# SwiGLU's upward products of two blocks in seven half-depth products instead of eight

## The chip, the cores and the metric

One Trainium2 chip, one core. The time is device microseconds of one launch; the median of three runs of the kernel before is 3152.8 us (3152.46 to 3155.65). Names as in the profile: PE is TensorE, DVE VectorE, ACT ScalarE, POOL GpSimd, SP the engine that issues most transfers.

## The reference, cut to what matters

A trunk of two layers; each layer has a SwiGLU, a mixer, and a second SwiGLU, so four SwiGLUs in all. 576 time steps (512 of the prompt and 8 x 8 samples), width 1024, inner width 2816 = 22 blocks of 128.

```
def swiglu(h, w1, w3, w2):
    return (jax.nn.silu(h @ w1) * (h @ w3)) @ w2
...
h = modulate(rms_norm(x, w['g_ffn1']), sh1, sc1)
x = x + 0.5 * gt1 * swiglu(h, w['w1_a'], w['w3_a'], w['w2_a'])
```

All is float32. The change is in h @ w1 and h @ w3, the upward products.

## The kernel before, in words

A float32 product is made of three matmuls on values split in two: hi (rounded to the engine's short form) and lo (the rest); hi x hi, hi x lo, lo x hi (`three`, lines 203 to 212). The time axis lies in two halves of 288 columns (HB), so one matmul is 128 x 128 weights by 128 x 288 of h, and `run` (line 214) adds the 8 depth tiles of one half in one bank.

Weights come block by block: `pump` (line 123) issues the transfer of a raw tile (128 x 1024, three in flight, line 142), casts it to hi on ScalarE (line 161), and puts off the subtraction that gives lo to VectorE (line 121, `rest`). WB = 5 split tiles may live at a time, AHEAD = 4 sets how early a tile is split. The order of use is a list of steps with their keys, filled by `ffn`; transfers are issued in the order of the keys.

`pair_step` takes one block: for each time half, w1's product, w3's product, then `post`: silu on ScalarE (line 611), the multiply on VectorE (line 612), and the split of the result g into hi and lo (lines 225 and 226). The blocks go in three groups (GROUPS: 6, 8 and 8); behind each group, `down` multiplies its g with the rows of w2 that belong to it, eight tiles of output, and adds to x (lines 581, 584, 587, 590). Between the steps of the first two SwiGLUs stand the units that make the conditioning values (`ada_unit`, line 277), two behind each block until they are used up. `end` takes the last four downward tiles, with the next normalization's statistics between them, and `begin` the first two blocks of a SwiGLU. Each engine works through its own queue in the order in which the program was written down.

Of the kernel before, what the change touches and what calls it, by code (L numbers as in the profile page):

```python
# [21 lines left out]
FT = 22  # L23
GROUPS = ((0, 6), (6, 8), (14, 8))
# [5 lines left out]
RAW, WB, AHEAD, ADA = 3, 5, 4, 12  # L30
# [5 lines left out]
SLOTS, TEMPS = 38, 12  # L36
# [26 lines left out]
class Trunk:  # L63
    def __init__(self, nc, tc, d, o, ctx):
        self.nc, self.tc, self.d, self.o = nc, tc, d, o
        pool = lambda name, **k: ctx.enter_context(tc.tile_pool(name=name, **k))
        self.cp = pool("const", bufs=1)
        self.wp = pool("weights", bufs=1)
        self.sp = pool("slots", bufs=SLOTS)
        self.tp = pool("temps", bufs=TEMPS)  # L70
        self.pp = pool("psum", bufs=1, space=PSUM)
        self.dp = pool("dram", bufs=1, space=bass.MemoryType.DRAM)
        self.n = 0
        self.steps = []
        self.spare = set()
        self.bg = deque()
        self.taps = 3
        self.later = []
        self.quota = 0
        self.ada_sb = None  # L80
# [29 lines left out]
    def start(self):  # L110
        self.keys = [k for ks, _ in self.steps for k in ks]
        self.at = {k: i for i, k in enumerate(self.keys)}
        assert len(self.at) == len(self.keys)
        self.order = np.cumsum([k[0] not in ("ada", "do") for k in self.keys]).tolist()
        self.raw, self.late, self.split = deque(), deque(), {}
        self.n_dma = self.held = self.whole = self.live = self.cur = 0
# [6 lines left out]
    def pump(self, later=False):  # L123
        nc = self.nc
        while True:
# [5 lines left out]
            elif self.n_dma < len(self.keys) and self.keys[self.n_dma][0] == "ada":  # L131
                if self.whole < ADA and self.n_dma <= self.cur + 2 * ADA:
# [14 lines left out]
            if self.raw and self.quota and self.order[self.raw[0][0]] <= self.order[self.cur] + AHEAD:  # L147
                key = self.keys[self.raw[0][0]]
                spare = key in self.spare
                if spare or self.live < WB:  # L150
# [17 lines left out]
            if not went:  # L168
                return

# [58 lines left out]
    def setup(self):  # L229
# [4 lines left out]
        self.one512 = cp.tile([128, 128], F32, name="one512")  # L234
# [10 lines left out]
        nc.gpsimd.memset(self.one512, 1.0 / 512)  # L245
# [181 lines left out]

    def end(self, keys, xs, post, last):
# [13 lines left out]
        for i, (k, w) in enumerate(zip(keys, ws)):  # L442
            ps = self.run(w, xs, 1, 0, {0: 4, 1: 6}.get(i), {0: stats, 1: spread}.get(i))
# [25 lines left out]
    def begin(self, l, sh, pairs, post):  # L469
# [24 lines left out]
        for pair in pairs:  # L494
            ps = self.outer([self.use(k) for k in pair], 1)
            for k in pair:
                self.free(k)
            self.pump()
            post(pair, 1, ps)
# [98 lines left out]
    def ffn(self, l, ab, sh, fill, first, last):  # L598
# [23 lines left out]
        if not first:  # L622
            self.spare |= {pairs[0][1], pairs[1][0]}

        def opening():
            if first:
                self.begin_first(l, sh, pairs[0], post)
            else:
                self.begin(l, sh, pairs[:2], post)
# [11 lines left out]

        def down(keys, final):
            f0, n = GROUPS[keys[0][3]]
# [14 lines left out]
        for gi, (f0, n) in enumerate(GROUPS):  # L658
            for f in range(f0, f0 + n):
# [4 lines left out]
                elif f > 1 or first:  # L664
                    self.steps.append((pairs[f], lambda f=f: pair_step(pairs[f])))
                    add_fill(0 if first and f == 5 else 2)
            final = gi == 2
# [12 lines left out]
    def mixer(self, l, last):  # L680
# [290 lines left out]
        def norm():  # L971
# [7 lines left out]
            for half in range(2):  # L979
                c = slice(half * HB, (half + 1) * HB)  # L980
                ps = self.mis(HB)
                nc.tensor.matmul(ps, self.one512, a[:, c], start=True, stop=True)
                for i in range(4):
                    nc.vector.tensor_sub(cvs[i][:, c], cvs[i][:, c], ps)
# [436 lines left out]
```

## Time and profile before

| | |
|---|---|
| median of three runs | 3152.8 us |
| profiled execution | 3153.93 us |
| its span | 3152.2 us |
| granted TensorE clock, mean | 0.993 |
| TensorE matmuls | 23412, busy 98% |
| VectorE, ScalarE, GpSimd busy | 49%, 28%, 13% |
| read from HBM | 328.9 MB, 108 GB/s over the span |

The busy share of TensorE is made of overlapping matmuls: one is listed at 0.29 us, and they follow each other every 0.13 us. What a matmul costs is therefore read from how many are issued in a stretch without waits, not from its duration.

### The profile page before, as it was taken

The page shows a single profiled execution, that of the slowest core. Times are in us where ns is not written, and L with a number is a line of the kernel's source. Part 1 is how long each engine was busy: PE and PEld are TensorE (multiplying, and loading weights), DVE is VectorE, ACT ScalarE, POOL GpSimd, SP SyncE. Part 2 cuts the span into 40 slices and gives each one's busy share as a digit, 9 for nine tenths or more (in the row PEclk, how much of TensorE's full clock was granted, in tenths as well). Part 3 has the DMA queues.
Part 4 walks back from the last instruction along what each step waited for, and adds up shares of the span by engine and source line. Part 5 has one row for each costly group of instructions (what it writes and reads, how often), then busy time and mean ns, then how long its engine had stood idle before and what let it go on. Part 6 is the DMA issues. An engine that isn't in the chain of part 4 may idle for free.

```text
span 3152.2 us, 55303 instructions
## 1 busy us (share of the span) xinstructions
PE 3096.1 (98%) x23412; PEld 2972.5 (94%) x23412; DVE 1533.6 (49%) x2840; ACT 874.4 (28%) x1468; POOL 407.0 (13%) x526
## 2 busy tenths in 40 slices
PE   7999999999999999999999999999999999999998
PEld 5999999899998999999999999988999899999998
DVE  5333335355995463323363333454679854533334
ACT  4222223222232342222232222332223333422221
POOL 1000004223212020000020000042221220200000
PEclk9999999999999999999999999999999999999999
DMA  7544424325322334636322222233352233222221
GB/s 275 166 154 151 151 88 129 111 68 124 86 75 69 119 121 146 207 126 218 109 79 79 84 87 85 84 123 111 83 113 86 70 101 92 75 89 81 81 82 57
DMA packets 142680, 349.67 MB, mean 111 GB/s; under 512 B 32400, under 2 KB 36752, under 8 KB 142432
## 3 DMA queue, kind: packets, MB, share of 16 engines
q1 hardware_dynamic: 135776, 329.35, 33.2%
q0 software_dynamic: 5504, 15.61, 1.8%
q8 instruction: 183, 3.00, 0.4%
q10 hardware_dynamic: 1152, 1.18, 0.1%
q14 instruction: 65, 0.53, 0.1%
HBM read 328.90 MB, written 12.45 MB: 108 GB/s over the span
## 4 chain that ended last, share of the span: by engine, by line
PE 95%; POOL 2%; DVE 1%; DMA 1%; ACT 0%; issue 0%; ACTq 0%; SPq 0%; POOLq 0%; DVEq 0%
PE pl L210 29%; PE pl L211 28%; PE pl L212 28%; PE pm L277 2%; PE pl L765 1%; PE pl L767 1%; PE pl L766 1%; PE pm L1164 1%; PE pm L1166 1%; DMA ada<-in_ada 1%; DVE hl L383 0%; DVE t L393 0%; PE pm L350 0%; DMA x<-in_x 0%; PE pm L1145 0%
## 5 line engine op out<-in xcount | busy, mean ns | idle before, releaser
L211 PE MATMUL pl<-hl,hi 128*128 128x288 f32 x4576 | 1348.9, 295 | 11.0 <-POOL hl L421 9.6
L210 PE MATMUL pl<-hh,hi 128*128 128x288 f32 x4576 | 1358.7, 297 | 0.3 <-ACT hh L419 0.2
L212 PE MATMUL pl<-hh,lo 128*128 128x288 f32 x4576 | 1348.1, 295 | 0.0
L210 PEld LDWEIGHTS pl<-hh,hi 128*128 128x128 f32 x4576 | 858.9, 188 | 21.5 <-DVE t L612 10.7
L211 PEld LDWEIGHTS pl<-hl,hi 128*128 128x128 f32 x4576 | 859.0, 188 | 13.8 <-POOL hl L421 10.9
L212 PEld LDWEIGHTS pl<-hh,lo 128*128 128x128 f32 x4576 | 858.8, 188 | 0.0
L121 DVE TENSOR_TENSOR lo<-raw,hi 128x1024 fp32r<-128x1024 f32 (+1 forms) x446 | 551.5, 1238 | 517.5 <-ACT hi L161 517.3
L161 ACT CAST hi<-raw 128x1024 fp32r<-128x1024 f32 (+1 forms) x446 | 459.1, 1032 | 849.9 <-PE pl L211 639.4
L210 PE MATMUL pl<-ghi,hi 128*128 128x288 f32 x1408 | 419.5, 298 | 0.0
L212 PE MATMUL pl<-ghi,lo 128*128 128x288 f32 x1408 | 414.7, 295 | 0.0
L211 PE MATMUL pl<-glo,hi 128*128 128x288 f32 x1408 | 414.6, 294 | 0.0
L590 POOL TENSOR_TENSOR xs<-xs,t 128x64 f32<-128x64 f32 x112 | 42.2, 377 | 1831.8 <-DVE t L587 1831.6
L210 PEld LDWEIGHTS pl<-ghi,hi 128*128 128x128 f32 x1408 | 264.1, 188 | 13.6 <-issue 11.5
L612 DVE TENSOR_TENSOR t<-t,pl 128x288 f32<-128x288 f32 x176 | 79.9, 454 | 404.8 <-PE pl L212 390.2
L211 PEld LDWEIGHTS pl<-glo,hi 128*128 128x128 f32 x1408 | 264.2, 188 | 0.0
L212 PEld LDWEIGHTS pl<-ghi,lo 128*128 128x128 f32 x1408 | 264.1, 188 | 0.0
L210 PE MATMUL pl<-s,hi 128*128 128x288 f32 x768 | 229.3, 299 | 0.0
L211 PE MATMUL pl<-s,hi 128*128 128x288 f32 x768 | 227.9, 297 | 1.1 <-DVE s L226 1.1
L212 PE MATMUL pl<-s,lo 128*128 128x288 f32 x768 | 227.8, 297 | 0.0
L957 DVE SCALAR_TENSOR_TENSOR cv<-up,vec,cv 128x512 f32<-128x512 f32 x240 | 209.2, 872 | 5.4
L225 ACT CAST ghi<-t 128x288 fp32r<-128x288 f32 x176 | 76.1, 432 | 481.0 <-DVE t L612 481.0
L210 PEld LDWEIGHTS pl<-s,hi 128*128 128x128 f32 x768 | 145.8, 190 | 3.3 <-issue 1.5
(197 smaller groups left out, 2689.2 us busy)
## 6 DMA issues: line engine op xcount, KB each, us to landing
ada<-in_ada SPq DMA_DIRECT2D x288, 256.0 KB, 4.5
raw<-in_win SPq DMA_DIRECT2D x120, 512.0 KB, 3.6
raw<-in_w1a SPq DMA_DIRECT2D x44, 512.0 KB, 3.6
raw<-in_w3a SPq DMA_DIRECT2D x44, 512.0 KB, 3.7
raw<-in_w1b SPq DMA_DIRECT2D x44, 512.0 KB, 3.6
raw<-in_w3b SPq DMA_DIRECT2D x44, 512.0 KB, 3.6
raw<-in_w2a SPq DMA_DIRECT2D x32, 512.0 KB, 3.5
raw<-in_w2b SPq DMA_DIRECT2D x32, 512.0 KB, 3.5
```

The lines of the kernel that those rows point to most:

```text
L121: self.nc.vector.tensor_sub(lo, t, hi.bitcast(F32))
L161: nc.scalar.copy(hi[:, :m], t[:, c])
L210: mm(ps[:, :HB], hi[:, c], x[0][:, t], start=first, stop=False)
L211: mm(ps[:, :HB], hi[:, c], x[1][:, t], start=False, stop=False)
L212: mm(ps[:, :HB], lo[:, c], x[0][:, t], start=False, stop=last)
L225: nc.scalar.copy(hi, src)
L277: nc.tensor.matmul(self.ps_ada[32 * j:32 * j + 32, :], self.cs[:, k], w, start=(k == 0), stop=(k == 7))
L590: nc.gpsimd.tensor_add(xs, xs, t[:].rearrange("p b t -> p (b t)"))
L612: nc.vector.tensor_mul(s, s, ps[1][:, :HB])
L765: mm(ps, xh, wh, start=(k == 0), stop=False)
L766: mm(ps, xh, wl, start=False, stop=False)
L957: nc.vector.scalar_tensor_tensor(cv[:, :S], up[:, k:k + S], w[:, k:k + 1], cv[:, :S], ALU.mult, ALU.add)
```

## The change

From the fifth block on, two blocks f and f + 1 are taken together, first for w1 and then for w3. Of the 2 x 2 scheme (two blocks by two halves of the depth, two halves of the depth by two halves of time) seven products of half the depth are made instead of eight (`seven`). For that the weights' quarters are summed on GpSimd (`sums`): from the raw tiles a and b come X (a itself), S (half as wide), Y and Z, and each is split into hi and lo like a weight tile before. The sums and differences of h are made once in each SwiGLU (`forms`, and `last_forms` just before the first pair of blocks, which writes over h's second time half of the first four depth tiles). The seven results are joined by VectorE on the way out. w1's four results stay in four temporaries until the w3 step. The silu's multiply is on VectorE for one of the four results and on GpSimd for three.

The groups are now four (6, 6, 4, 6 blocks), raw tiles four instead of three, temporaries 10 instead of 12, slots 37 instead of 38, and conditioning tiles in flight 4 instead of 12 once the start is over. A block of ones that held 1/512 is gone; its factor is applied on VectorE.

```
-GROUPS = ((0, 6), (6, 8), (14, 8))
+GROUPS = ((0, 6), (6, 6), (12, 4), (16, 6))
-RAW, WB, AHEAD, ADA = 3, 5, 4, 12
+RAW, WB, AHEAD, ADA, ADA_LATER = 4, 5, 4, 12, 4
-SLOTS, TEMPS = 38, 12
+SLOTS, TEMPS = 37, 10
...
+            if self.jobs:
+                if not (later and once) and self.live + self.jobs[0][0] <= WB:
+                    self.jobs.popleft()[1]()
+                    if not later:
+                        self.rest()
+                    went = once = True
...
+    def halves(self, key, t, n=1024):
+        w = [self.wp.tile([128, 1024], F32R, tag=x, bufs=WB, name=self.name(x)) for x in ("hi", "lo")]
+        self.live += 1
+        self.nc.scalar.copy(w[0][:, :n], t[:, :n])
+        self.late.append((w[1][:, :n], t[:, :n], w[0][:, :n]))
+        self.split[key] = w
+    def sums(self, key, a, b):
+        add = self.nc.gpsimd.tensor_add
+        s = self.wp.tile([128, 512], F32, tag="s1", bufs=1, name=self.name("s1"))
+        add(s, b[:, :512], b[:, 512:])
+        add(b[:, :512], b[:, :512], a[:, :512])
+        def z():
+            self.rest()
+            add(a[:, :512], a[:, :512], s)
+            add(a[:, 512:], a[:, 512:], a[:, :512])
...
+        self.jobs.extend(((1, lambda: self.halves((*key, "X"), a)), (0, z),
+                          (1, lambda: self.halves((*key, "S"), s, 512)), (1, yh), (1, zh)))
...
+    def last_forms(self):
+        for i, z in enumerate(self.zs):
+            hi, lo = self.T[7][i]
+            self.nc.scalar.copy(hi, z[:, HB:])
+            self.nc.vector.tensor_sub(lo, z[:, HB:], hi.bitcast(F32))
...
+    def seven(self, key, post):
...
+        p, q = bank(), bank()
+        product(p, "X", 0, quarter(0, 0), True, True)
+        s1 = self.temp([128, HB])
+        nc.scalar.copy(s1, p)
+        self.rest()
+        product(q, "Y", 0, self.T[7], True, True)
+        u, v = self.temp([128, HB]), s1
+        nc.vector.tensor_add(u, s1, q)
+        self.rest()
+        product(p, "X", 1, quarter(1, 0), False, True)
+        free("X")
+        post(0, 0, p)
+        self.rest()
+        product(q, "Z", 0, self.T[2], False, True)
+        nc.vector.tensor_sub(v, s1, q)
+        nc.vector.tensor_sub(u, u, q)
+        self.rest()
+        r = bank()
+        product(r, "S", 0, self.T[5], True, True)
+        free("S")
+        post(1, 1, v, r)
+        self.rest()
+        t = bank()
+        product(t, "Y", 1, self.T[4], True, True)
+        free("Y")
+        post(1, 0, v, t)
+        self.rest()
+        product(r, "Z", 1, quarter(1, 1), False, True)
+        free("Z")
+        post(0, 1, u, r)
+        self.rest()
...
+            def up3(i, j, a, b=None):
+                s = acts.pop((i, j))
+                if b is None:
+                    nc.vector.tensor_mul(s, s, a)
+                else:
...
+                    nc.gpsimd.tensor_mul(s, s, t)
+                c = slice(j * HB, (j + 1) * HB)
+                hi, lo = (x[:, c] for x in g[f + i])
+                nc.scalar.copy(hi, s)
+                waiting.append(lambda: nc.vector.tensor_sub(lo, s, hi.bitcast(F32)))
...
+                elif f > 3:
+                    for up in range(2 - f % 2 * 2):
+                        ks = [pairs[f][up], pairs[f + 1][up]]
+                        self.steps.append((ks, lambda f=f, up=up: duo_step(f, up)))
+                        add_fill(2)
```

`product` is four times three matmuls. A pair of blocks is so a w1 step and a w3 step of seven products each, numbered 1 to 7 in the order above.

ScalarE's queue, first, where one block follows another in the last SwiGLU. Before: hi is a weight's cast, t the silu's result, ghi the cast of g.

```order
L611 ACTIVATE t_31043<-pl_30991 128x288
L225 CAST ghi_31041<-t_31043 128x288
L161 CAST hi_31073<-raw_30867 128x1024
L611 ACTIVATE t_31104<-pl_31048 128x288
L225 CAST ghi_31041<-t_31104 128x288
L161 CAST hi_31109<-raw_30928 128x1024
```

After, where a w3 step ends and the next w1 step begins, without conditioning units between: L194 casts a weight part, L838 g, L542 copies the first product's bank, L816 is the silu.

```order
L194 CAST hi_33260<-raw_33015 128x1024
L838 CAST ghi_33041<-t_33145 128x288
L194 CAST hi_33283<-raw_32992 128x1024
L838 CAST ghi_33039<-t_33169 128x288
L194 CAST hi_33316<-raw_33131 128x1024
L542 COPY t_33331<-pl_33314 128x288
L816 ACTIVATE t_33362<-pl_33314 128x288
```

The last cast of g (L838) and the cast of the next X (L194) now stand between the end of one step and the copy (L542) that lets the next step's third product begin.

GpSimd's queue, before, at the opening and the first downward tiles of the last SwiGLU: L387 is a part of h, L590 adds to the samples' x.

```order
L421 TENSOR_TENSOR hl<-s_28398,hh 128x8x64
L387 TENSOR_TENSOR hl<-t_28449,hh 128x224
L387 TENSOR_TENSOR hl<-t_28471,hh 128x224
L387 TENSOR_TENSOR hl<-t_28479,hh 128x224
L590 TENSOR_TENSOR xs_104<-xs_104,t_29159 128x64
L590 TENSOR_TENSOR xs_104<-xs_104,t_29208 128x64
```

After, in the same SwiGLU at the end of that w3 step: L835 multiplies silu and gate, L204 and L205 are the first two sums of the next but one step's weights, L209 and L210 the other two.

```order
L835 TENSOR_TENSOR t_33124<-t_33124,t_33254 128x288
L835 TENSOR_TENSOR t_33145<-t_33145,t_33277 128x288
L204 TENSOR_TENSOR s_33288<-raw_33152 128x512
L205 TENSOR_TENSOR raw_33152<-raw_33152,raw_33131 128x512
L835 TENSOR_TENSOR t_33169<-t_33169,t_33303 128x288
L209 TENSOR_TENSOR raw_33131<-raw_33131,s_33288 128x512
L210 TENSOR_TENSOR raw_33131<-raw_33131 128x512
```

Between the blocks GpSimd had nothing before; now two sums stand between the second and the third multiply of the step, and two more behind it.

VectorE's queue at the same two places. Before, L612 multiplies, L226 gives g's lo and L121 a weight's lo.

```order
L612 TENSOR_TENSOR t_31043<-t_31043,pl_31016 128x288
L226 TENSOR_TENSOR glo_31042<-t_31043,ghi_31041 128x288
L121 TENSOR_TENSOR lo_31074<-raw_30867,hi_31073 128x1024
L612 TENSOR_TENSOR t_31104<-t_31104,pl_31079 128x288
L226 TENSOR_TENSOR glo_31042<-t_31104,ghi_31041 128x288
L121 TENSOR_TENSOR lo_31110<-raw_30928,hi_31109 128x1024
```

After, L832 and L834 join products of the w3 step, L839 gives g's lo, L129 a weight part's lo, L546 is the first join of the w1 step.

```order
L834 SCALAR_TENSOR_TENSOR t_33277<-t_33190,pl_33259 128x288
L839 TENSOR_TENSOR glo_33042<-t_33124,ghi_33041 128x288
L129 TENSOR_TENSOR lo_33261<-raw_33015,hi_33260 128x1024
L832 TENSOR_TENSOR t_33303<-t_33207,pl_33241 128x288
L839 TENSOR_TENSOR glo_33042<-t_33145,ghi_33041 128x288
L129 TENSOR_TENSOR lo_33284<-raw_32992,hi_33283 128x1024
L839 TENSOR_TENSOR glo_33040<-t_33169,ghi_33039 128x288
L129 TENSOR_TENSOR lo_33317<-raw_33131,hi_33316 128x1024
L546 TENSOR_TENSOR t_33348<-t_33331,pl_33315 128x288
```

Four subtractions with both operands in SBUF, two of them 1024 wide, now stand between the last join of one step and the first join of the next.

## Rows read from the trace of the kernel before

**Rows 1.** the page: busy time and share of each engine; granted clock by slice.
```profile
PE 3096.1 (98%) x23412; PEld 2972.5 (94%) x23412; DVE 1533.6 (49%) x2840; ACT 874.4 (28%) x1468; POOL 407.0 (13%) x526
PEclk9999999999999999999999999999999999999999
```

**Rows 2.** the page: the chain that ended last, shares of the span.
```profile
PE 95%; POOL 2%; DVE 1%; DMA 1%; ACT 0%; issue 0%; ACTq 0%; SPq 0%; POOLq 0%; DVEq 0%
```

**Rows 3.** waits of TensorE: us in total, times, longest us.
```profile
PE pl L211 <- POOL hl L421: 9.6, 6, 1.8
PE pm L336 <- DVE ssq L369: 7.6, 6, 4.7
```

**Rows 4.** 60 us of SwiGLU: busy us (instructions) per engine, clock, DMA share, GB/s.
```profile
1660.00:1720.00 60.00, 60.00 (x455) 60.00 (x454) 20.28 (x32) 15.77 (x28) 0.32 (x1) 1.00 0.24 71
```

**Rows 5.** groups by form: count | busy us, mean ns | idle before, releaser.
```profile
L121 DVE TENSOR_TENSOR lo<-raw,hi 128x1024 fp32r<-128x1024 f32 x414 | 520.3, 1258 | 492.1 <-ACT hi L161 491.8
L121 DVE TENSOR_TENSOR w<-raw,w 128x512 fp32r<-128x512 f32 x20 | 12.5, 685 | 0.0
L161 ACT CAST hi<-raw 128x1024 fp32r<-128x1024 f32 x414 | 432.4, 1047 | 779.8 <-PE pl L211 599.7 <-PE pl L761 56.7 <-issue 35.6
L161 ACT CAST w<-raw 128x512 fp32r<-128x512 f32 x20 | 10.9, 616 | 0.0
L612 DVE TENSOR_TENSOR t<-t,pl 128x288 f32<-128x288 f32 x176 | 79.9, 454 | 404.8 <-PE pl L212 390.2 <-ACT t L611 14.5
L225 ACT CAST ghi<-t 128x288 fp32r<-128x288 f32 x176 | 76.1, 432 | 481.0 <-DVE t L612 481.0
L611 ACT ACTIVATE t<-pl 128x288 f32<-128x288 f32 x176 | 71.6, 407 | 169.1 <-PE pl L212 169.1
L369 POOL TENSOR_TENSOR ssq<-ssq,t 128x288 f32<-128x288 f32 x18 | 14.6, 810 | 1.4
L415 POOL TENSOR_TENSOR s<-s,ada 128x512 f32<-128x512 f32 x5 | 6.4, 1279 | 0.4
L411 POOL TENSOR_TENSOR s<-xs,t 128x512 f32<-128x512 f32 x5 | 9.0, 1810 | 23.1 <-ACT t L409 23.1
```

**Rows 6.** timeline, GpSimd and VectorE, two stretches: start, us, engine, line.
```profile
513.16 1.27 POOL L415 TENSOR_TENSOR s<-s,ada 128x512 f32<-128x512 f32 x1
514.39 1.64 POOL L387 TENSOR_TENSOR hl<-t,hh 128x224 fp32r<-128x224 f32 x1
...
513.41 2.10 DVE L121 TENSOR_TENSOR lo<-raw,hi 128x1024 fp32r<-128x1024 f32 x1
...
518.46 0.97 POOL L704 TENSOR_TENSOR s<-t,t 128x288 f32<-128x288 f32 x1
...
518.69 0.79 DVE L393 SCALAR_TENSOR_TENSOR t<-x,ada,pm 128x224 f32<-128x224 f32 x2
...
532.59 1.33 DVE L121 TENSOR_TENSOR lo<-raw,hi 128x1024 fp32r<-128x1024 f32 x1
...
532.79 1.79 POOL L706 TENSOR_TENSOR s<-t,t 128x288 f32<-128x288 f32 x1
```

**Rows 7.** the chain in order of time, 1283 to 1320: start, us, what.
```profile
1284.64 1.00 PE pm L277 x16
```

**Rows 8.** stretches behind five SwiGLU openings, columns as in rows 4.
```profile
517.30:523.30 6.00, 4.93 (x35) 4.70 (x36) 4.21 (x10) 2.46 (x6) 6.00 (x8) 1.00 0.17 64
1175.20:1181.20 6.00, 6.00 (x45) 6.00 (x46) 3.73 (x10) 4.45 (x12) 2.01 (x3) 1.00 0.66 248
1645.00:1651.00 6.00, 6.00 (x34) 6.00 (x35) 3.45 (x9) 3.18 (x8) 2.05 (x3) 0.72 0.15 59
2071.30:2077.30 6.00, 5.96 (x32) 5.61 (x33) 4.21 (x10) 2.46 (x6) 6.00 (x8) 0.72 0.19 70
2729.50:2735.50 6.00, 6.00 (x46) 6.00 (x47) 3.72 (x10) 4.47 (x12) 2.01 (x3) 1.00 0.15 59
1645.90:1649.30 3.40, 3.40 (x16) 3.40 (x15) 2.09 (x6) 2.74 (x8) 1.32 (x2) 0.50 0.05 22
```

More of the change, by code (lines that the diff above doesn't have):

```diff
@@ L124, in pump @@
         nc = self.nc
+        once = False
         while True:
@@ new lines, in last_forms, with product @@
+    def last_forms(self):
[3 more added lines that the diff above has]
+            self.nc.vector.tensor_sub(lo, z[:, HB:], hi.bitcast(F32))
+        self.zs = None
+    def seven(self, key, post):
+        nc = self.nc
+        mm = nc.tensor.matmul
+        h = [(x[0][:, :NT], x[1]) for x in self.h]
+        quarter = lambda k, j: [(x[0][:, j * HB:(j + 1) * HB], x[1][:, j * HB:(j + 1) * HB]) for x in h[4 * k:4 * k + 4]]
+        def product(ps, which, at, xs, first, last):
+            hi, lo = self.part(key, which)
+            for i, x in enumerate(xs):
+                c = slice(512 * at + 128 * i, 512 * at + 128 * i + 128)
+                k = dict(skip_group_check=True)
+                mm(ps, hi[:, c], x[0], start=first and i == 0, stop=False, **k)
+                mm(ps, hi[:, c], x[1], start=False, stop=False, **k)
+                mm(ps, lo[:, c], x[0], start=False, stop=last and i == 3, **k)
+        bank = lambda: self.lin(HB)
+        free = lambda which: self.free((*key, which))
+        p, q = bank(), bank()
[29 more added lines that the diff above has]
+        self.rest()
@@ L467, in outer, with begin @@
         return ps
-    def begin(self, l, sh, pairs, post):
+    def begin(self, l, sh, pairs, post, forms=()):
         st = {}
@@ L493, in begin @@
         post(pairs[1], 0, self.outer(ws, 0, {0: spread, 1: first, 3: more, 5: more}))
-        for pair in pairs:
-            ps = self.outer([self.use(k) for k in pair], 1)
+        forms = iter(forms)
+        more = lambda: next(forms, None)
+        for n, pair in enumerate(pairs):
+            hooks = {k: more for k in (1, 3, 5)}
+            ps = self.outer([self.use(k) for k in pair], 1, hooks)
             for k in pair:
@@ L622, in ffn @@
         if not first:
-            self.spare |= {pairs[0][1], pairs[1][0]}
+            self.spare |= {pairs[0][1]}
+        for f in range(4, FT, 2):
+            for i in range(2):
+                self.duo[pairs[f][i]] = pairs[f + 1][i]
         def opening():
@@ L628, in opening @@
             else:
-                self.begin(l, sh, pairs[:2], post)
+                forms = self.forms()
+                self.begin(l, sh, pairs[:2], post, forms)
+                self.bg.append(forms)
         def pair_step(pair):
@@ L663, in ffn @@
                     self.steps.append((ks, opening))
[L664 to L667, printed above, removed]
+                elif f > 3:
[3 more added lines that the diff above has]
+                        add_fill(2)
+                elif first or f > 1:
+                    self.steps.append((pairs[f], lambda f=f: one_pair(f)))
+                    add_fill(2)
+            final = gi == len(GROUPS) - 1
             if final:
```

104 lines of the change are left out of this document (95 added, 9 removed).

## Prediction

> **What bounds the kernel now.** I read the page's table of engines and slices first: TensorE is busy 98% of the span and every slice is granted full clock [rows 1]. The reader is to see that no engine but TensorE is near its limit. Then the chain of waits: 95% of it is TensorE [rows 2]. Third, TensorE's own waits: at the openings of a SwiGLU it waits 9.6 us in six times, for statistics 7.6 us [rows 3], so nearly the whole run is matmul issue. Fourth, 60 us of plain SwiGLU work: 455 matmuls in 60.00 us at clock 1.00, so one 288-column matmul costs 60.00/455 = 0.132 us [rows 4]. A kernel bound like this gets faster only by fewer matmuls, and only as long as what replaces them stays out of TensorE's way.
>
> **What it removes.** A pair of blocks took 2 blocks x 2 time halves x 8 depth tiles x 3 = 96 matmuls for w1 and as many for w3. Seven products of 4 depth tiles x 3 are 84. Nine pairs of blocks x 2 weights x 4 SwiGLUs are 72 steps, each 12 matmuls shorter: 864 x 0.132 = **114.0 us**. A step is 84 x 0.132 = 11.1 us, one product P = 12 x 0.132 = 1.58 us.
>
> **What it adds.** Per step VectorE splits three weight tiles of 1024 and one of 512 (X, Y, Z, S) instead of two of 1024; ScalarE casts the same. GpSimd makes four sums of 128x512 per step, and in the w3 step three products of 128x288. VectorE joins products: three ops before and three in the evictions. Prices: split 1.23 to 1.26 us for 1024 and 0.69 for 512; casts 1.05 and 0.62; 288-wide ops 0.45 on VectorE, 0.41 to 0.43 on ScalarE, 0.81 on GpSimd [rows 5]. The sum of 128x512 with plain operands isn't in the trace. Nearest rows: 1.28 for one that met little, 1.81 for one that met a split [rows 5]. I take 1.28, which the 288-wide add bears out (0.81 x 512/288 = 1.44, an upper bound since its fixed part is scaled too), and keep 1.8 as the upper end.
>
> By busy time this fits: GpSimd 8 x 1.28 + 3 x 0.81 = 12.7 of 22.2 us a pair, VectorE some 16, ScalarE some 12. It doesn't fit by order. Two facts make it late, and a third makes lateness dearer.
>
> *First, VectorE and GpSimd exclude each other.* A split that started 0.25 us after a GpSimd op took 2.10 us and ended 1.08 us after that op had; the GpSimd op behind it took 1.64 us for a 224-wide subtract. In the other direction a GpSimd 288-wide op that met a split took 1.79 us and ended 0.66 us after the split. VectorE ops that read one operand from PSUM ran at their usual pace (two in 0.79 us) beside a GpSimd op [rows 6]. So the splits (raw and hi, both in SBUF) and the lo parts of g must take turns with the sums; the joins need not. The Trainium skill, "SBUF — State Buffer", section "Who interferes with whom", says the same of VectorE instructions with two SBUF inputs, and that the other engine blocks for the whole instruction; by that rule no collision is cheaper than a whole instruction, and the trace agrees with 2.10 and 1.79 us.
>
> *Second, the opening of a w1 step hangs on the end of the w3 step before.* The third product adds onto the bank that ScalarE must first copy (line 542 of the new code). ScalarE's queue has in front of that copy the cast of the last g tile and the cast of the next X; the g cast waits for GpSimd's last product, and where no conditioning unit stands between the steps, two sums stand in front of that product. The order of both queues at this place stands in the section on the change.
>
> I walk it with zero at the start of a w3 step that waits 0.2 us at its opening. Products 5, 6, 7 end at 8.1, 9.7, 11.3; a result is seen 0.3 us later. Join of product 6: 10.0 to 10.45. GpSimd's multiply, after the lo part of g that is ready at the same moment: 11.65. Split of Y: 12.75. First sum: 14.0. lo part: 14.4. Second sum: 15.65. Split of Z: 16.75. Last multiply: 17.5. g cast (0.43): 18.0. X cast (1.05): 19.05. Copy (0.41) and hand-over: 19.5. The third product of the w1 step could start at 11.3 + 2P = 14.45. It stands **5.1 us** late. With the shorter prices that the collisions show (1.08 and 0.66) it is 4.7, with Z's split behind the multiply 3.7; without any exclusion (multiply of product 6 done at 11.3, sums 13.95, last multiply 14.8, copy 16.7) 2.3. I take 4.2. What is late next, the join for the fourth product (behind X's split, 20.65), is hidden behind it.
>
> Where two conditioning units (1.00 us of matmuls [rows 7]) stand between, the sums come behind the last multiply: copy at 16.3 against 15.45, 0.9 late, and then X's split waits for both sums, so that the fourth product stands 2.0 more. I take 2.6 (0.3 without exclusion, 3.5 at most).
>
> The groups hold 1, 3, 2 and 3 pairs of blocks, so 0 + 2 + 1 + 2 = 5 such openings in each SwiGLU, 20 in all. The units run out in the last group of the first two SwiGLUs: 6 openings with units, 14 without. 14 x 4.2 = **58.8**; 6 x 2.6 = **15.6**.
>
> *Third, the clock.* At five openings TensorE stands some 1.8 us [rows 3]. After two of the five the granted clock is at the lower level, 1.2 GHz, for part of the next 6 us (mean 0.72, 0.50 in the slowed stretch: 34 and 32 matmuls where full clock has 45 and 46); after the other three it stays at 1.00, 2.4 GHz [rows 8]. One drop costs about 11.5 x 0.132 = 1.5 us. A stand of 4.2 us is longer, so I take seven of ten of the 14: 14 x 0.7 x 1.5 = **15** (6 at the least, 30 if all 20 drop).
>
> *Small terms, together 14* (5 to 35). A w3 step's opening waits too: its copy stands behind the X cast, 0.2 x 24 steps without units = 5. The first downward run after a group needs g of the last products: 0.2 us for groups of six and 1.5 for the group of four, about 5 in all. Casting the difference of the halves over h just before block 5: 2. The last four downward tiles run 6 instead of 8 deep, so the statistics chain behind them has 2.4 instead of 3.2 us per run; it waits 7.6 us in all now [rows 3], plus 0.7 x 4 = 3.
> At nothing I cost the forms of h (in the opening and blocks 3 and 4, where VectorE is busy 20 of 60 us [rows 4]; 16 ops of 0.45 and 4 twice as wide make 11 us a SwiGLU, the cost if that cover were gone), the evictions of the fourth group (VectorE, beside TensorE's 1.6 us runs), and four conditioning tiles in flight instead of twelve (uncovered up to 10 us in the second SwiGLU). A gain of TensorE's on any of these I exclude: none shortens its stream.
>
> **The sum.** -114.0 + 58.8 + 15.6 + 15 + 14 = -10.6. The profiled execution took 3153.9 us (span 3152.2), 1.1 over the median of 3152.8. It is the same work in both, so I take the difference off the median: **3142 us**.
>
> **Rivals.**
> *The exclusion matters little* (GpSimd's sums fall into VectorE's pauses). For it: VectorE is busy half the time [rows 1]. Against: splits and sums are released by the same events. Stands 14 x 2.3 + 6 x 0.3 = 34, clock 14 x 0.4 x 1.5 = 8, small terms 5: -67, **3086**.
> *Slower: each sum takes 1.8 us*, the row that meets a split. Place: GpSimd's two sums ahead of the last multiply, and those ahead of Y's split in the w1 step. Openings of w1 steps lose 1.0 more x 20, the 24 openings of w3 steps without units 1.0 more: +44, **3186**. It decides from about 1.4 us a sum on (13 us of the 44). For it: in the walk the first sum stands behind Y's split and the second behind a lo part. Against: the walk has these waits in it already.
> *Every stand drops the clock.* By the rows, 20 x 1.5 = 30 instead of 15: **3157**, no change. The Trainium skill, "TensorE: Matmul & The Clock Gate", section "HAM oscillation — how this bites in real kernels", describes work that starts cold after each idle gap; the trace has it in two of five gaps.
>
> **Numbers.** Forecast 0.45 (own range 3122 to 3165), little exclusion 0.18, slow sums 0.27, clock each time 0.10. The range, 3085 to 3188, reaches from the case of little exclusion to that of slow sums, since either alone holds about a fifth of the chance or more; beyond its ends I leave some 2 in 10, for lesser stands below and more clock drops above. About 0.2%, 6.3 us, is what a measurement can tell from no change. The forecast gives 0.28 faster, 0.09 same, 0.08 slower; little exclusion 0.17 and 0.01; slow sums 0.03, 0.03, 0.21; clock 0.02, 0.05, 0.03. Together 0.50, 0.18, 0.32.
>
> **What would show it.** Matmuls 864 fewer; TensorE waiting at the third product of w1 steps for ScalarE's copy, 14 times 4 us and 6 times 1 us, and at the fourth for VectorE; GpSimd's sums well over 1.3 us in the mean; clock digits of 8 and 9 in SwiGLU slices. It is wrong if TensorE's waits sum to under 50 us or over 130, if they sit in the w3 steps, or if the DMA queue appears as what ended them.

## The result and the profile after

The changed kernel takes 3321.5 us (median of four, 3315.6 to 3323.8), beside 3153.7 for the kernel before on the same chip: ratio 1.053, interval 1.051 to 1.055. Forecast were 3142 us. It is slower by 168 us where a small gain was expected, and lies above the whole range.

The page first, the rows that answer to [rows 1]:

```profile
PE 3072.1 (93%) x22548; PEld 2928.9 (88%) x22548; DVE 1981.4 (60%) x3545; ACT 1033.6 (31%) x1761; POOL 1013.0 (31%) x985
PEclk9999999999999999898998999999999999989999
```

TensorE makes 864 matmuls fewer, as counted, and its busy share falls from 98 to 93%. No engine has become a bound by its busy time: VectorE is at 60%. Four slices show the clock below nine tenths.

TensorE's waits, answering to [rows 3] (us in total, times, longest):

```profile
PE pl L533 <- ACT t L542: 65.3, 17, 5.8
PE pm L348 <- DVE t L337: 53.5, 17, 13.1
PE pl L267 <- ACT t L758: 23.0, 4, 8.1
PE pm L391 <- DVE ssq L424: 16.1, 9, 4.7
...
PE pl L533 <- ACT hh L517: 14.6, 3, 7.0
...
PE pl L533 <- DVE t L546: 6.7, 5, 1.6
...
PE pl L267 <- ACT hi L180: 5.8, 7, 1.3
PE pl L269 <- DVE lo L129: 4.7, 9, 0.7
```

The first row is, in 14 of its 17 times, the wait that was forecast; the rows on lines 348 and 758 weren't, and line 517 only with 2 us. All rows together are 239 us, where the kernel before has 48. Next the four SwiGLUs by stretch (length, busy us and count of each engine, clock, DMA share, GB/s):

```profile
27.60:544.70 517.10, 466.10 (x3530) 426.85 (x3530) 297.70 (x509) 166.37 (x290) 183.34 (x165) 0.96 0.42 141
1203.30:1754.70 551.40, 475.73 (x3572) 440.49 (x3571) 286.48 (x495) 161.08 (x276) 175.44 (x159) 0.92 0.39 130
1754.70:2205.70 451.00, 414.19 (x2978) 410.96 (x2979) 284.71 (x471) 158.88 (x276) 175.72 (x159) 0.95 0.26 80
2862.70:3308.00 445.30, 408.28 (x2954) 404.34 (x2953) 276.06 (x460) 152.01 (x261) 174.08 (x157) 0.96 0.23 73
```

Before, the same four took 477.5, 469.7, 426.4 and 423.2 us at clock 1.00; the second of them:

```profile
1162.60:1632.30 469.70, 467.66 (x3788) 440.36 (x3787) 174.52 (x319) 120.64 (x201) 25.14 (x44) 1.00 0.46 153
```

They lose 39.6, 81.7, 24.6 and 22.1; the mixers between are unchanged to 1.2 us. The second SwiGLU, which has conditioning units between nearly all its steps, loses half of the 168 us.

To size the parts I took the interval between the starts of successive matmuls in both traces: up to 1.25 times what is usual for its line it is plain issue, up to 2.15 times it is a matmul at the lower clock, above that a stand, time in which TensorE does nothing. Differences, after minus before, in us:

| | forecast | measured |
|---|---|---|
| matmuls | -114.0 | -115.1 |
| w1 openings without units (third product) | 58.8 | 58.3 = 14 x 4.16 |
| w1 openings with units | 15.6 | 7.0 = 4 x 1.74 |
| w1 openings behind downward tiles | 0 | 12.2 |
| slow clock behind stands | 15 | 66.3 |
| conditioning transposes, line 348 | 0 | 59.0 |
| splits behind units in downward tiles | 0 | 12.7 |
| silu of blocks 0 to 3 (line 758) | 0 | 24.0 |
| last forms, lines 517 and 518 | 2 | 20.9 |
| first pair of the first SwiGLU, a weight late | 0 | 5.9 |
| statistics at the end | 3 | 8.8 |
| rest | 9 | 7.9 |
| sum | -10.6 | 167.9 |

Of the six openings with units, none stands at the third product; four stand at the fourth, for VectorE's join (line 546), two not at all. The 5.9 us look like the last forms, since they come at the same place, but there ScalarE's queue waited for a transfer of w3:

```profile
223.66 0.40 PE L533 MATMUL pl<-thi,hi 128*128 128x288 f32 x1 [1.57 <-DVE t L546]
...
113.55 1.04 ACT L194 CAST hi<-raw 128x1024 fp32r<-128x1024 f32 x1 [6.19 <-DMA raw<-in_w3a]
```

One opening of the third SwiGLU, timeline (start, us, engine, line, idle time before and its releaser):

```profile
1905.48 0.46 DVE L834 SCALAR_TENSOR_TENSOR t<-t,pl 128x288 f32<-128x288 f32 x1 [0.75 <-PE pl L535]
...
1906.84 1.26 DVE L129 TENSOR_TENSOR lo<-raw,hi 128x1024 fp32r<-128x1024 f32 x1 [0.49 <-ACT hi L194]
...
1908.03 0.44 DVE L832 TENSOR_TENSOR t<-t,pl 128x288 f32<-128x288 f32 x1
...
1909.50 2.30 DVE L129 TENSOR_TENSOR lo<-raw,hi 128x1024 fp32r<-128x1024 f32 x1
...
1912.48 0.43 ACT L838 CAST ghi<-t 128x288 fp32r<-128x288 f32 x1 [4.04 <-POOL t L835]
1912.82 1.04 ACT L194 CAST hi<-raw 128x1024 fp32r<-128x1024 f32 x1
1913.76 0.39 ACT L542 COPY t<-pl 128x288 f32<-128x288 f32 x1
...
1906.98 2.28 POOL L204 TENSOR_TENSOR s<-raw 128x512 f32<-128x512 f32 x1
1909.33 1.38 POOL L205 TENSOR_TENSOR raw<-raw,raw 128x512 f32<-128x512 f32 x1
1910.67 1.77 POOL L835 TENSOR_TENSOR t<-t,t 128x288 f32<-128x288 f32 x1
...
1914.20 0.61 PE L533 MATMUL pl<-hh,hi 128*128 128x288 f32 x1 [4.00 <-ACT t L542]
```

Read it from the bottom: TensorE waits 4.00 us for the copy, that stands behind two casts, the first of them waits 4.04 us for GpSimd's multiply, and that stands behind two sums: its input, the join of line 832, was ready at 1908.47, and it began at 1910.67. The first sum met Y's split and took 2.28 us; Z's split met the second sum and took 2.30; the multiply met Z's split and took 1.77. The forecast's walk put the end of the copy 9.5 us behind the join of the sixth product; here it is 8.7 behind (1905.48 to 1914.15).

Behind the stand the clock falls (columns as above), and this happened behind all 14:

```profile
1914.20:1920.00 5.80, 5.80 (x33) 5.80 (x34) 2.15 (x5) 0.92 (x2) 2.55 (x2) 0.72 0.11 43
```

In these 5.8 us 33 matmuls begin where full clock has 44. Over the 14 the slow matmuls cost 1.3 to 2.8 us each, 1.9 in the mean. In the trace's record of the clock there are 42 stretches at 1.2 GHz, 244 us together, where the kernel before has 6 and 44 us. Behind the four stands of 1.74 us at openings with units it did not fall.

The prices, answering to [rows 5] (count | busy us, mean ns | idle before):

```profile
L204 POOL TENSOR_TENSOR s<-raw 128x512 f32<-128x512 f32 x72 | 122.2, 1697 | 149.8 <-DVE lo L129 53.5 <-DMA raw<-in_w1b 42.0 <-DMA raw<-in_w3a 26.8
L205 POOL TENSOR_TENSOR raw<-raw,raw 128x512 f32<-128x512 f32 x72 | 109.1, 1515 | 5.6
L210 POOL TENSOR_TENSOR raw<-raw 128x512 f32<-128x512 f32 x72 | 100.9, 1402 | 5.6
L209 POOL TENSOR_TENSOR raw<-raw,s 128x512 f32<-128x512 f32 x72 | 95.3, 1324 | 189.1 <-DVE lo L129 140.6 <-issue 47.0
```

One sum takes 1.48 us in the mean (427.5 / 288), between the 1.28 taken and the 1.8 of the slower rival. Now the wait that the prediction left out, for a conditioning result, first as it was:

```profile
PE pm L293 <- DVE t L282: 0.5, 1, 0.5
```

That row is from the kernel before, where it waits 0.5 us in all for such copies. After, in the second SwiGLU:

```profile
1425.63 1.07 PE L332 MATMUL pm<-ada,cs 128*32 128x256 f32 x16
1431.07 0.69 PE L348 MATMUL pm<-ident,t 128*128 128x128 f32 x2 [4.37 <-DVE t L337]
...
1427.44 1.81 DVE L129 TENSOR_TENSOR lo<-raw,hi 128x1024 fp32r<-128x1024 f32 x1
1429.17 1.51 DVE L839 TENSOR_TENSOR glo<-t,ghi 128x288 fp32r<-128x288 f32 x1
1430.61 0.41 DVE L337 COPY t<-pm 128x256 f32<-128x256 f32 x1
```

TensorE asks for the transposes at once behind the units; the copy that they need stands in VectorE's queue behind the backlog of the w3 step. And the forms of h in the third SwiGLU:

```profile
1793.66 1.28 POOL L209 TENSOR_TENSOR raw<-raw,s 128x512 f32<-128x512 f32 x1 [11.88 <-issue]
...
1796.26 1.41 POOL L491 TENSOR_TENSOR za<-hh,hl 128x576 f32<-128x576 f32 x1
...
1797.70 1.63 DVE L495 TENSOR_TENSOR za<-za 128x288 f32<-128x288 f32 x1 [4.17 <-POOL za L491]
...
1804.42 0.61 PE L267 MATMUL pl<-hh,hi 128*128 128x288 f32 x1 [7.17 <-ACT t L758]
```

The sums of h (line 491) stand on GpSimd behind the weights' sums, which had to wait for X's split; the forms then come all at once, the first three subtractions 1.5 to 1.6 us each beside a sum instead of 0.46, and the silu waits in ScalarE's queue behind a cast of their result.

### The profile page after: what moved, and what is told of

Its sections match the earlier page's. It is cut to its first block, busy times and chain, and to the rows that moved or that the text cites. A ratio compares the mean times of both kernels' runs of the same rounds, so it can differ in the third digit from the quotient of the medians.

```text
span 3320.0 us, 55694 instructions
## 1 busy us (share of the span) xinstructions
PE 3072.1 (93%) x22548; PEld 2928.9 (88%) x22548; DVE 1981.4 (60%) x3545; ACT 1033.6 (31%) x1761; POOL 1013.0 (31%) x985
## 5 line engine op out<-in xcount | busy, mean ns | idle before, releaser
L129 DVE TENSOR_TENSOR lo<-raw,hi 128x1024 fp32r<-128x1024 f32 (+2 forms) x553 | 704.0, 1278 | 424.1 <-ACT hi L180 330.4
L267 PE MATMUL pl<-hh,hi 128*128 128x288 f32 x2320 | 695.9, 300 | 23.6 <-ACT t L758 23.0
L268 PE MATMUL pl<-hl,hi 128*128 128x288 f32 x2320 | 689.5, 297 | 9.1 <-POOL hl L476 6.4
L269 PE MATMUL pl<-hh,lo 128*128 128x288 f32 x2320 | 688.4, 297 | 1.5 <-DVE lo L129 1.5
L180 ACT CAST hi<-raw 128x1024 fp32r<-128x1024 f32 (+2 forms) x337 | 315.9, 944 | 590.0 <-PE pl L268 316.1
L267 PEld LDWEIGHTS pl<-hh,hi 128*128 128x128 f32 x2320 | 440.2, 190 | 31.3 <-ACT t L758 23.9
L268 PEld LDWEIGHTS pl<-hl,hi 128*128 128x128 f32 x2320 | 440.1, 190 | 12.3 <-POOL hl L476 7.7
L533 PE MATMUL pl<-hh,hi 128*128 128x288 f32 x1152 | 363.2, 315 | 84.7 <-ACT t L542 65.3
L269 PEld LDWEIGHTS pl<-hh,lo 128*128 128x128 f32 x2320 | 439.7, 190 | 1.9 <-DVE lo L129 1.9
L534 PE MATMUL pl<-hl,hi 128*128 128x288 f32 x1152 | 357.5, 310 | 4.6 <-DVE hl L518 4.6
L535 PE MATMUL pl<-hh,lo 128*128 128x288 f32 x1152 | 357.5, 310 | 1.6 <-DVE lo L129 1.6
L533 PEld LDWEIGHTS pl<-hh,hi 128*128 128x128 f32 x1152 | 232.4, 202 | 98.3 <-ACT t L542 69.3
L194 ACT CAST hi<-raw 128x1024 fp32r<-128x1024 f32 x216 | 224.4, 1041 | 158.8 <-PE pl L268 89.9
L737 POOL TENSOR_TENSOR xs<-xs,t 128x64 f32<-128x64 f32 x144 | 65.4, 455 | 648.2 <-DVE t L734 644.8
L534 PEld LDWEIGHTS pl<-hl,hi 128*128 128x128 f32 x1152 | 233.4, 203 | 5.6 <-DVE hl L518 5.6
L535 PEld LDWEIGHTS pl<-hh,lo 128*128 128x128 f32 x1152 | 233.1, 202 | 2.1 <-DVE lo L129 2.1
```

Of the source, the lines that this page charges most:

```text
L129: self.nc.vector.tensor_sub(lo, t, hi.bitcast(F32))
L180: nc.scalar.copy(hi[:, :m], t[:, c])
L194: self.nc.scalar.copy(w[0][:, :n], t[:, :n])
L267: mm(ps[:, :HB], hi[:, c], x[0][:, t], start=first, stop=False)
L268: mm(ps[:, :HB], hi[:, c], x[1][:, t], start=False, stop=False)
L269: mm(ps[:, :HB], lo[:, c], x[0][:, t], start=False, stop=last)
```

## The experiments

The theories have letters. A is mostly the queues: each late result stands behind a sum, a transfer or a split that could come later. B is mostly the exclusion itself: VectorE has too much to do beside the sums wherever they stand. C is about line 348: it is asked for with no work in between. D and E concern the transfers. What A and B mean in a run, its expectation says. Ratios are to the kernel before, with their 95% intervals; the changed kernel's is 1.053 [1.051, 1.055].

**The last multiply.**

```
-                    nc.gpsimd.tensor_mul(s, s, t)
+                    nc.vector.tensor_mul(s, s, t)
```

> The silu's multiply in the w3 steps (line 835) goes from GpSimd to VectorE; nothing else changes. Theory A (the last g of a w3 step waits for GpSimd's multiply, which stands behind two sums, and ScalarE's copy for the next w1 step waits behind that g's cast): the 14 stands of 4.16 us at the openings of w1 steps shrink to 1.5 us or less, and the slow clock that follows each of them (some 1.9 us) goes for most: 14 x (2.7 to 4.2) + 14 x 1 to 1.9 = 50 to 85 us off 3321, about 3236 to 3271. Theory B (the exclusion of VectorE and GpSimd decides: the joins and splits themselves come late because sums run beside them, wherever the multiply is): the stands lose at most 1 us each and the clock drops stay, 3300 to 3321.

Measured 3260.3 us, 1.033 [1.032, 1.035]: 61 us off, as A says. The 14 stands are 1.14 us each, and in front of each there is now one of 0.6 us in the second product, at the lo of its weight part Y. One opening, on TensorE and VectorE:

```profile
1885.29 0.40 PE L535 MATMUL pl<-hh,lo 128*128 128x288 f32 x1 [0.42 <-DVE lo L129]
...
1880.37 1.03 DVE L835 TENSOR_TENSOR t<-t,t 128x288 f32<-128x288 f32 x1
1881.32 1.55 DVE L839 TENSOR_TENSOR glo<-t,ghi 128x288 fp32r<-128x288 f32 x1
```

The sums now lengthen the multiply (0.46 alone) and a lo part (0.45 alone) on VectorE, by 1.67 us together, about as much as the two stands. That what is left is exclusion is read from this, not tested by itself.

**Weights past the conditioning tiles.** In `pump`, while a conditioning tile waits for its limit:

```
+                elif self.quota > 9:
+                    i = self.n_dma
+                    while i < len(self.keys) and (self.keys[i][0] == "ada" or i in self.early):
+                        i += 1
+                    if i < len(self.keys) and self.keys[i][0] != "do" and self.held < RAW:
+                        self.load(i)
```

> Weight tiles may be issued past conditioning tiles that are held back by the limit of four; the conditioning tiles themselves keep their limit. Theory A (the limit of four stops the one list of transfers, so weights arrive late in the first two SwiGLUs, and the copy of the conditioning result waits in VectorE's queue behind splits that wait for weights and sums): TensorE's stands at line 348 (59 us) fall to under 20, those behind units and for splits (20 us) to under 8, and with the clock some 15 more: 50 to 75 us off 3321, 3246 to 3271; the third and fourth SwiGLU don't change. Theory B (the transfers are in time, and the copy stands behind splits that wait for GpSimd's sums anyway): line 348 keeps over 40 us, 3300 to 3321.

Measured 3312.1 us, 1.050 [1.048, 1.051], which can't be told from the changed kernel for certain. Line 348 (here 362) fell only to 38.8 us, and another wait came:

```profile
PE pm L362 <- DVE t L351: 38.8, 17, 7.4
PE pm L346 <- DMA ada<-in_ada: 28.2, 17, 8.2
```

The second SwiGLU gained 20 us, the first lost 11: weights that go ahead in the same queue hold up the conditioning tiles. By its time and by line 348 the run is near theory B, which had over 40 us there and 3300 to 3321, but the new wait stands in neither theory.

**The sums of h first.** The eight sums of lines 491 and 492 in a loop of their own before the first `yield` of `forms`.

> All eight GpSimd sums of h (lines 491, 492) are issued before the first part of the forms instead of two at a time between the blocks, so none of them stands behind the weights' sums. Theory A (the third and fourth part of the forms come 10 us late since their sums stand in GpSimd's queue behind weights' sums that wait for a split, and then hold up VectorE and ScalarE in blocks 2 and 3): the stands on the silu of these blocks (6, 2, 7.3 and 8.2 us) go, those for the last forms (5.9, 7.2, 6.0, 5.6) go by half, with clock 6 more: 30 to 45 us off, 3276 to 3291. Theory B (the work of the forms is too much for VectorE in these blocks whenever it comes): the stands move to other lines and the time stays within 10 us of 3321.

Measured 3313.0 us, 1.050 [1.048, 1.052]: B's side. The stands at the silus fell from 24.0 to 14.5 us, those at the first pair of blocks (the last forms and the late weight) rose from 26.8 to 31.0.

**The kernel before with four conditioning tiles.**

```
-                if self.whole < ADA and self.n_dma <= self.cur + 2 * ADA:
+                if self.whole < (ADA if self.quota < 9 else 4) and self.n_dma <= self.cur + 2 * ADA:
```

> The kernel before with at most four conditioning tiles in flight after the start instead of twelve, nothing else. Theory A (the limit alone starves the weights): the first two SwiGLUs become 20 to 60 us longer, 3173 to 3213. Theory B (the limit costs only where splits wait for sums): TensorE's waits grow by under 8 us, 3153 to 3161.

Measured 3154.3 us, 1.000 [0.999, 1.001]. By itself, in the kernel before, the limit costs nothing; theory A of this run fell.

**Without the weights' sums.** The four adds are taken out of `sums`, and S is split from `a[:, :512]`, so this kernel multiplies by other weights.

> The four sums of the weights' parts (lines 204, 205, 209, 210) are left out; Y, Z and S are split from the raw tiles as they are, so the products are those of other weights. All transfers, casts, splits, joins and matmuls stay. It prices all that the sums do. Theory A (the sums are the root: they hold up the last multiply and, by excluding VectorE, the splits, and so also the conditioning copy behind them): stands at openings of w1 steps under 0.5 us, those at line 348 under 10 in all, forms a little sooner: 120 to 170 us off 3321, 3150 to 3200. Theory C (the conditioning result is asked for, at line 348, with no work between it and the copy, so the stand stays however fast the queues are): line 348 keeps 30 us or more with some 10 of clock, 3195 to 3235.

Measured 3191.4 us, 1.012 [1.010, 1.013]: 130 us off. With no sum at all the w1 openings still stand 1.25 us, and line 348 (here 342) keeps two thirds:

```profile
PE pm L342 <- DVE t L331: 37.3, 17, 7.3
```

So the sums cost 130 us in all, more than the matmuls they save. The time lies in theory A's range, but both stands are above what A allowed: line 348 is mainly C's.

**The transposes later.**

```
         free("X")
+        self.ada_done()
         post(0, 0, p)
```

and the calls at the start of `duo_step` and of the downward tiles (lines 808 and 857) go, but for the last four tiles.

> The transposes of a conditioning result (line 348) are issued inside a step, behind the third product, instead of at its start, and in the downward tiles behind the first time half. Theory C (line 348 is asked for too early; the copy is there some 2 to 5 us later in any case): its 59 us of stands fall under 10 in all, with 20 us of clock: 55 to 80 off 3321, 3241 to 3266, all in the first two SwiGLUs. Theory B (VectorE is that much behind at these places, so the next thing that needs it, the first join of the step or an eviction, stands instead): the stands go to lines 533 to 535 and 267, 0 to 25 us off, 3296 to 3321.

Measured 3279.6 us, 1.040 [1.038, 1.041]: 42 us off, between the two. Line 348's stands fell to 6.8 us, nearly all in one place, but the two rows below it

```profile
PE pm L348 <- DVE t L337: 6.8, 3, 5.9
PE pl L267 <- ACT hi L180: 11.1, 10, 1.3
PE pl L533 <- DVE t L546: 10.4, 9, 1.6
```

were 5.8 and 6.7: part of the time went to the next thing that VectorE or a transfer had late.

**Four edits together.** The three above (multiply, transposes, sums of h) and `last_forms` right behind block 3's last product instead of behind its silu.

> Four edits together: the multiply on VectorE, the conditioning transposes inside the step, the sums of h first, and the last forms (lines 517, 518) issued before block 3's silu instead of behind it. If the causes are separate, the gains add: 61 + 55 to 80 + 8 + about 15 of the 25 us at the last forms, 140 to 165 off 3321: 3156 to 3181, about no change against the kernel before, since what remains (the openings' 1.7 us, blocks 2 and 3, the clock behind the remaining stands) is still as large as the matmuls saved. If all come from one backlog on VectorE, moving the multiply there takes back part of the others: 3200 to 3235.

Measured 3202.4 us, 1.015 [1.014, 1.017]. That is 119 off, the sum of the three measured alone (61 + 42 + 8) and 8 more. By the expectation's numbers that is the range of one backlog, but only because it took 55 to 80 us for the transposes where 42 were measured; the gains measured alone add up. The last two SwiGLUs take 425.0 and 419.2 us, as long as before or less; the second still takes 514.2 instead of 469.7.

**Conditioning tiles from ScalarE's queue**, with the look-ahead of the second experiment:

```
-                    nc.sync.dma_start(self.split[key], self.source(key)[0])
+                    queue = nc.sync if self.quota < 9 else nc.scalar
+                    queue.dma_start(self.split[key], self.source(key)[0])
```

> The four edits of e7_all, and after the start the conditioning tiles are issued from ScalarE's queue instead of SP's, so that weights aren't queued behind transfers that wait for a conditioning unit of TensorE, and weights may be issued past conditioning tiles that the limit of four holds back. Theory D (what is left in the second SwiGLU, 44 us more than before, is weights that arrive late because they share one queue with the conditioning tiles): its stands before and in downward tiles (18 us), at line 348 (8 us) and at two openings (7 us) go for the most part, with some 10 us of clock: 20 to 35 us off 3202, 3167 to 3182. Theory E (weights are late since a raw tile is held until the last of its sums is split, whatever queue the transfer is in): under 8 us off, 3194 to 3206.

Measured 3171.9 us, 1.004 [1.003, 1.006]: 30 us off, theory D (one of its four runs took 3159.4). The second SwiGLU went from 514.2 to 486.5 us. In the kernel with four edits SP's queue waits for conditioning units of TensorE (first row), and GpSimd's first sum of a step for weights (second row); now the first wait is gone from SP's queue, and the sum (here line 219) waits for weights 6.2 us:

```profile
SPq L144 <- PE pm L332: 327.5, 61, 23.4
L204 POOL TENSOR_TENSOR s<-raw 128x512 f32<-128x512 f32 x72 | 103.3, 1435 | 158.4 <-DVE lo L129 67.2 <-DMA raw<-in_w1b 35.3 <-DMA raw<-in_w3a 27.8
...
L219 POOL TENSOR_TENSOR s<-raw 128x512 f32<-128x512 f32 x72 | 98.6, 1369 | 115.1 <-DVE lo L130 108.9 <-DMA raw<-in_w1a 6.2
```

Which of the two edits carries it was not tried apart on this kernel. Both leave the limit at four, so what the limit itself costs beside the sums is open too.

**The lo parts of g later.** `duo_step` hands its last three lo parts to the next w1 step:

```
         nc.vector.tensor_add(u, s1, q)
+        self.carried()
         self.rest()
```

> As e9_act_queue, and where a w3 step is followed by a w1 step without units between, the lo parts of the last three g tiles are put behind the first join of that w1 step, and the other one behind the last multiply, so VectorE makes the next weights' lo first. Theory A (VectorE's backlog at the openings, lengthened by lo parts of g that meet GpSimd's sums: one took 1.55 instead of 0.45 us): the 14 openings' 1.14 and 0.58 us go, with half a clock drop each: 20 to 30 us less than e9_act_queue. Theory B (the collisions move on to the weights' splits, which are longer): within 6 us of e9_act_queue.

Measured 3153.7 us, 1.000 [0.999, 1.001], 18 us less than the run before; at the 14 openings the stands of 0.6 and 1.14 us are one of 0.67. Theory A, a little smaller than expected. Here the whole loss is undone.

**Block 3's time halves swapped**, with `last_forms` between them.

> As e10_carry, and block 3 takes its second time half first, so that the last forms, which write over that half of h, have the first half's 6.3 us of matmuls to hide behind. Theory A (the stands at the first pair, 7.1, 6.6, 4.7 and 4.0 us in e7_all, are these casts and subtractions alone): 15 to 25 us less than e10_carry, and the whole 3130 to 3150, faster than the kernel before. Theory B (they are the backlog of VectorE in blocks 2 and 3, of which the last forms are only the end): the stands move into block 3's second half, within 6 us of e10_carry.

Measured 3153.3 us, 1.000 [0.999, 1.001]. A fell: in the third SwiGLU the stands at the first pair are some 5 us instead of 4.4, and most of them moved from the second product to the third. So they are not the last forms' casts and subtractions alone; a backlog, theory B, fits.

**Seven products from the seventh block on.** `range(6, FT, 2)` for `range(4, FT, 2)`, `elif f > 5` for `elif f > 3`, and the forms made in the ticks of blocks 2 to 5.

> As e10_carry, but seven products only from the seventh block on (eight pairs of blocks instead of nine), and the forms of h are made tick by tick in blocks 2 to 5 instead of in the opening and blocks 2 and 3. It costs 4 x 24 matmuls more, 12.7 us. Theory A (the stands in blocks 2 and 3 and at the last forms, some 4 + 4.5 us in each of the last two SwiGLUs of e10_carry and more in the first two, with two or three clock drops, are a backlog of VectorE that a longer stretch takes up): 20 to 35 us in all, 3119 to 3134 after the 12.7 us are paid, faster than the kernel before. Theory B (the forms cost the same wherever they are, since they meet splits and sums there too): 3150 to 3167.

Measured 3126.5 us, 0.990 [0.989, 0.992]: faster than the kernel before by 28.7 us, in theory A's range. The third SwiGLU, clock 1.00 again (columns as above), and its waits:

```profile
1640.10:2049.40 409.30, 401.57 (x3002) 398.70 (x3001) 283.78 (x482) 154.82 (x270) 132.01 (x124) 1.00 0.28 88
```

```profile
PE pl L556 <- ACT t L565: 3.4, 7, 0.6
PE pm L407 <- DVE ssq L440: 3.3, 2, 2.7
```

It saves 192 matmuls instead of 216 and takes 17 us less than before; nothing stands in blocks 2 to 5. The forms, begun later and spread over four blocks, no longer hold TensorE up. But something else changed with them: the first pair of blocks now comes behind the first group's downward tiles, and so the weights' sums don't begin until these tiles, behind all forms (the last forms' casts end at 1715.5):

```profile
1736.66 1.29 POOL L220 TENSOR_TENSOR s<-raw 128x512 f32<-128x512 f32 x1
```

Whether the longer stretch or the absence of the weights' sums cures it, no run tells apart. The second SwiGLU still takes 479.3 us, 9.6 more than before; the gain is in the last two (35 us) and the first (4).

**The second SwiGLU block by block.** A flag for it at the two ranges of the edit above.

> As e12_from6, and the second SwiGLU, the one with units between all its steps, takes all 22 blocks one by one as in the kernel before. It makes 192 matmuls more, 25.3 us. If the units and the seven products still get in each other's way there (stands for conditioning tiles and at openings, 30 us with 15 us of clock in e10_carry), it comes out 0 to 10 us less than e12_from6; if e12_from6 has cleared them already, 10 to 25 us more.

Measured 3122.0 us, 0.990 [0.988, 0.991]. That is 4.5 us below the run above, and the intervals overlap: in the second SwiGLU, 192 matmuls fewer (25 us) buy about nothing.

## Why the prediction was wrong

*The step that failed* is the list of the other places where TensorE would wait. The prediction gave them 14 us (its own terms add up to 15) and put the forms, the transfers and the fourth group at nothing; the wait at line 348 and the openings behind downward tiles it didn't name at all. Together they measured 151 us: 59.0 at line 348, 44.9 at the forms, 12.7 at splits in downward tiles, 12.2 at openings behind downward tiles, 5.9 at a late weight, 16.7 in the rest. Behind it comes the clock, 66 us for 15. By its own sign it was wrong from 130 us of waits on; TensorE's waits are 239 us.

*The matmuls.* Right: 864 fewer, 115.1 us.

*The openings.* Right in place, cause and size: 14 stands of 4.16 us where 4.2 were taken, at the third product, for ScalarE's copy, behind GpSimd's last multiply. That the size came out to 0.05 us is partly luck, since 4.2 was taken from variants of the walk between 2.3 and 5.1. The first experiment shows that it hangs on the multiply on GpSimd. For the six openings with units the walk was half right: the fourth product stood 1.74 us, in four of them, where 2.0 were taken, the third not at all, 7.0 us for 15.6. The Trainium skill's rule ("SBUF — State Buffer", "Who interferes with whom") agrees with the collisions read here: the first sum, 1.28 us alone, ended 1.16 us behind the end of Y's split, and Z's split, 1.23 alone, 1.09 behind the end of the second sum. The prediction's reading of it, that no collision is cheaper than a whole instruction, is a little too dear: these two lost 1.00 and 1.07 us, beside operations of 1.26 and 1.38.

*The clock, a term that was too small.* Taken: seven of ten stands at 1.5 us, from five openings of 1.8 us [rows 8]. Measured: every one of the 14, at 1.9 us, 27 us; the other 39 of the 66 us come mostly behind stands that were not forecast. A rate read at stands of 1.8 us was carried to stands of 4.2; in the same trace none of the four stands of 1.74 us drops the clock. The page of the Trainium skill that the prediction set against its own rate, "TensorE: Matmul & The Clock Gate", section "HAM oscillation — how this bites in real kernels", where work starts cold after each idle gap, was nearer; the trace agrees with it behind these 14, and not behind the four of 1.74 us. The rival that built on it was right for the 14, and still far too low, since it had only the 20 openings.

*"At nothing I cost the forms of h."* They measured 24.0 us at the silus and 20.9 at the last forms. The prediction gave the price if the cover were gone, 11 us a SwiGLU, and then didn't hold it; 44.9 us are 11.2 a SwiGLU. It counted VectorE's idle time over 60 us, and not what the forms' sums do: on GpSimd they stand behind the weights' sums, and beside VectorE they lengthen its subtractions (1.63 us for 0.46). The last but one experiment takes the stands away, with a longer stretch and with the weights' sums out of it, which were not tried apart; an earlier place in GpSimd's queue alone (third experiment), or the swapped halves around the last forms, did not.

*A wait that the prediction left out*, the largest. The changed kernel asks for a conditioning result's transposes at the start of a step (lines 808 and 857), where the kernel before asked behind a product. That is 59.0 us in the first two SwiGLUs (53.5 in the rows of waits). Moving it takes 42 off, clock included, and the fifth experiment shows that 37.3 us stay even without any sum.

*Four conditioning tiles "at nothing".* True in the kernel before (fourth experiment). Beside the sums the conditioning transfers do cost: 30 us went when they got a queue of their own and weights could pass them, once the other causes were out of the way. Whether the limit of four has a part in it is open. The prediction said that it would be wrong if the DMA queue appeared as what ended the waits; on TensorE it has 1.4 us, but it stands one step behind, in front of casts and sums (the 6.19 us above, and 68.8 us in the row of line 204).

*The rivals.* The slower one had the sums at 1.8 us and put its cost at both kinds of openings. They took 1.48, and the openings of w3 steps didn't stand. It was on the right side by luck, for another reason. All rivals shared one base, the forecast's list of places; none of them was a place that the list left out, and there the loss was.

## What to carry to other kernels

When a change trades TensorE's work for work on other engines, list every instruction that TensorE waits for, the small ones too (a copy for a transpose, the reading of a result from its bank), and ask for each what now stands in its engine's queue: the busy share says nothing about it. Give a stand its clock as well: here each of 4.2 us cost 6.1. And place the added work where there is room: the seven products went from 5% slower to 1% faster, with one pair of blocks fewer, the multiply on the other engine, the waits moved behind a product, the conditioning transfers in a queue of their own, the lo parts of g later, and the preparation begun later, clear of the weights' sums.

## What the runs showed of the hardware

In the collisions read here, of VectorE and GpSimd operations with two operands in SBUF each, the later one was lengthened by about 1 us, whether it was long or short: a split of 128x1024 took 2.30 instead of 1.23 us, a subtraction of 128x288 1.63 instead of 0.46 beside a sum of 128x576. Short operations lose the larger share.

The granted clock fell to 1.2 GHz behind each of the 14 stands of 4.16 us and behind none of the four of 1.74 us.

A transfer that waits in a queue for TensorE was followed by late weights behind it: SP's queue waited 327.5 us for conditioning units, and the sums 63.1 us for weights, although the DMA engines moved only 130 GB/s in the second SwiGLU of the changed kernel, where the kernel before moved 153. With the conditioning tiles in ScalarE's queue and weights allowed past them, the sums waited 6.2 us.
